# Four-tile scalings on VectorE, half of the inversion's loads from GpSimd, and other planner prices for SyncE, in a gated DeltaNet and S5 trunk

## The chip, the cores and the metric

The kernel runs on one core of a Trainium2 chip. The metric is the device time of one execution in microseconds. TensorE (PE) does the matmuls, VectorE (DVE) and ScalarE (ACT) the element-wise work, GpSimd (POOL) small element-wise work, memsets and some DMAs, and SyncE (SP) only issues DMAs. The engines run their own instruction lists in order and meet at semaphores.

## The reference, cut to what matters

The model has two layers. The first is the one that the change touches: a gated DeltaNet mixer with 8 heads of 128 channels over 1024 tokens, in chunks of 64, beside a memory attention, then an output projection, a layer norm and an MLP. Per head, with gc the cumulated log decay in a chunk:

```python
diff = gc[..., :, None] - gc[..., None, :]
decay = jnp.where(causal, jnp.exp(jnp.where(causal, diff, 0.0)), 0.0)
a_strict = jnp.where(strict, jnp.einsum('bhnid,bhnjd->bhnij', kb, k) * decay, 0.0)
sol = lax.linalg.triangular_solve(eye + a_strict, rhs, left_side=True, lower=True, unit_diagonal=True)
def step(state, inp):
    v_new = ui - jnp.einsum('bhcd,bhde->bhce', wi, state)
    attn = jnp.einsum('bhid,bhjd->bhij', qi, ki) * deci
    o = qi*exp(gci) @ state + attn @ v_new
    state = state * exp(g_last) + k_dec^T @ v_new
```

The second layer has an S5 state-space mixer in place of the DeltaNet, then the same attention, projection, norm and MLP. All matrices are float32.

## The kernel before, in words

A large float32 product is split into a high and a low float32r part on each side and done as three matmuls (lines 371 to 373); ACT makes the high part of a weight (L350) and DVE the low one (L351), from a raw tile that SP loads (L341). Small products are float32 matmuls. The tokens lie in 8 tiles of 128 rows; a "half" is four of them, so that a tile [128, 4, 128] is half a head.

The DeltaNet runs over heads. `gdn_recur(h)` is the serial recurrence: per token tile a chain ks (L1308) to R on DVE (L1310), pe (L1314) to e, copied by ACT (L1316), pS (L1320) to S on DVE (L1325). Beside it runs `gdn_fill(h + 1)`, which supplies the filling matmuls: the projections of head h + 1 and the keys of head h + 3, each as 24 matmuls of 128x512 per half.

For each half, `gdn_keys_out` makes the decay tile D: `decay` (L987 to L997) loads the cumulated sums, adds the causal mask on DVE (L994) and exponentiates on ACT, tile by tile with the token's own sum as the bias (L996). ACT sums squares for the norms (L1017), scales the keys to kd (L1026, stored to kdd, L1027) and scales D by gam, four tiles (L1029), stored to ded (L1030). DVE multiplies D with the key product kk (L1036) to NT (L1037), and ACT copies its diagonal blocks to pkd (L1041); GpSimd stores NT and pkd. `gdn_values_out` scales the transposed values by sk, four tiles on ACT (L1224).

For each pair of heads `gdn_inverse` inverts the 32x32 diagonal blocks on DVE (L1067 to L1114), and GpSimd stores them to t32 (called t in the profile). Per head, `gdn_invert_tiles` (L1127 to L1188) loads them into seven tiles, bz (L1146), two thirds of mz (m1, L1148, and m3, L1153), bv (L1149), the two halves of tv (tA, L1151, and vB, L1154), na (L1156) and the two result tiles TT, called iv (L1158), 34 loads per head by SP, all but na of 32x4x32 elements; then five groups of four small matmuls (`mm4`, L1163) with copies between them. `gdn_fill` decides after how much of the projection work these five groups are emitted: for heads 2, 4 and 6 they are held back by `wait` (22.0, in the loop over heads in `run`).

`run` ends by `settle`, a list scheduler over the whole program after the first weight. It prices each instruction (`price`), walks the five engines' lists, and fixes the order on each engine. A DMA on SP costs 0.33 us of its queue and one on GpSimd 0.65 us in that table; a tile that is written anew can start when its buffer is free. PE may take an instruction up to 40 us ahead of the plan (`reach`). So any change of a price can move instructions of all engines.

Of the kernel before, what the change touches and what calls it, by code (L numbers as in the profile page):

```python
# [16 lines left out]
P = 128  # L17
# [13 lines left out]
class Trunk:  # L31
# [26 lines left out]
    def settle(self, first, last, reach=0.0, ahead=15.0, passes=1, margin=0.0, late=0.0, hold=1e3):  # L58
# [118 lines left out]
        for _ in range(passes):  # L177
            due, now = [0.0] * n, 0.0
            place = {x: k for k, x in enumerate(turns)}
            for x in turns:  # L180
                due[x] = now
                now += cost[x][0]
            for x in reversed(range(n)):
                if ins[x].engine != E.PE:
                    due[x] = min([due[y] for y in after[x] + next_[x]] + [now + 50.0]) - lag - cost[x][1]


            slots, turn = {}, {}
            for x in range(n):
                for nm in fresh[x]:  # L190
                    turn.setdefault(self.home[nm][:2], []).append(nm)
            for t in turn:
                held = sum(1 for nm in users if self.home[nm][:2] == t and nm in before)
                slots[t] = [0.0] * (self.home[turn[t][0]][2] - held)
            todo = {nm: len(s) for nm, s in users.items()}
            over = {nm: 0.0 for nm in users}

            def room(x):
                t0, need = 0.0, {}
                for nm in fresh[x]:  # L200
                    need.setdefault(self.home[nm][:2], set()).add(nm)
                for t, s in need.items():
                    if set(turn[t][:len(s)]) != s or len(slots[t]) < len(s):
                        return None
                    t0 = max(t0, sorted(slots[t])[len(s) - 1])
                return t0


            free, locked, served, head, kind = {e: 0.0 for e in names}, 0.0, 0.0, 0, ""
            ready, wait = [0.0] * n, [len(d | f) for d, f in zip(deps, follow)]  # L210
            open_ = {e: [x for x in range(n) if ins[x].engine == e and not wait[x]] for e in names}
            order, lost, gone, table = [], 0.0, set(), 0
            while len(order) < n:
                first_ = None
                drift = free[E.PE] - due[turns[head]] if head < len(turns) else 0.0
                for e in names:
                    pick = None
                    for x in open_[e]:
                        if e == E.PE and x != turns[head] and due[x] > due[turns[head]] + reach - 1e-6:
                            continue  # L220
                        s = room(x) if fresh[x] else 0.0
                        if s is None:
                            continue
                        r = max(ready[x], s, free[e], due[x] - ahead if e != E.PE else 0.0)
                        if cost[x][2] > 1.5:
                            r = max(r, due[x] + drift - hold)
                        if e == E.PE and kind == "fr" and ins[x].ins[0].dtype == F32:
                            r += 0.15
                        other = 1.28 if sets[x] not in (None, table) else 0.0
                        k = (0, due[x] + other, r, x) if r <= free[e] + 0.1 else (1, r + other, due[x], x)  # L230
                        if pick is None or k < pick[0]:
                            pick = k, r, x
                    if pick and (first_ is None or pick[1:] < first_[1:]):
                        first_ = pick
                assert first_, f"no order: {len(order)} of {n}"
                r, x = first_[1:]
                e = ins[x].engine
                busy, length, moves = cost[x]
                if sets[x] not in (None, table):
                    table, busy, length = sets[x], busy + 1.28, length + 1.28  # L240
                if moves:
                    served = max(served, r + length - moves) + moves
                    length = served - r + late
                if port[x]:
                    r = max(r, locked)
                    locked = r + busy
                if e == E.PE:
                    lost += r - free[e]
                    kind = (kind + "fr"[ins[x].ins[0].dtype == F32R])[-2:]
                    gone.add(x)  # L250
                    while head < len(turns) and turns[head] in gone:
                        head += 1
                open_[e].remove(x)
                free[e] = r + busy
                order.append(x)
                for nm in fresh[x]:
                    t = self.home[nm][:2]
                    slots[t].remove(min(slots[t]))
                    turn[t].remove(nm)
                for y in after[x] + then[x]:  # L260
                    same = e == E.PE and ins[y].engine == e
                    ready[y] = max(ready[y], r + (0.0 if x not in deps[y] else busy if same else length + lag + (margin if ins[y].engine == E.PE else 0.0)))
                    wait[y] -= 1
                    if not wait[y]:
                        open_[ins[y].engine].append(y)
                for nm in uses(ins[x]):
                    if nm in users:
                        over[nm] = max(over[nm], r + length)
                        todo[nm] -= 1
                        if not todo[nm] and nm not in behind and self.home[nm][:2] in slots:  # L270
                            slots[self.home[nm][:2]].append(over[nm] + lag)
            if best is None or free[E.PE] < best[0]:
                best = free[E.PE], order
            turns = [x for x in order if ins[x].engine == E.PE]
# [5 lines left out]
    def price(self, i, big):  # L280

        E = mybir.EngineType
        if i.opcode == "DMACopy":
            def run(ap):
                k = 1
                for s, c in reversed(ap):
                    if s != k:
                        break
                    k *= c
                return 4 * k  # L290

            q = [x.bass_ap.ap for x in (i.ins[0], i.outs[0])]
            size, k = 4e-3 * math.prod(c for s, c in q[1]), min(run(a) for a in q)
            moves = size / (300 if k >= 2048 else 230 if k >= 512 else 150 if k >= 256 else 90 if k >= 128 else 40)
            return (0.33 if i.engine != E.Pool else 0.65), 1.6 + size / 300 + (0.0 if k >= 512 else 0.7), moves
        if i.engine == E.PE:
            if i.ins[0].dtype == F32R:
                return 0.014 + 0.416e-3 * big, 0.39 if big > 256 else 0.29, 0
# [690 lines left out]
    def decay(self, h, hf, tag):  # L989

        nc = self.nc
        pb = self.sums(h, hf, tag)
        d = self.tile(tag, [P, 4, P], F32, "D")
        nc.vector.tensor_tensor(d, pb, self.maskneg.unsqueeze(1).to_broadcast([P, 4, P]), op=ALU.add)  # L994
        for t in range(4):
            nc.scalar.activation(d[:, t, :], d[:, t, :], AF.Exp, bias=self.ngc[:, 4 * hf + t, h:h + 1])  # L996
        return d  # L997

    def gdn_keys(self, h, xT, w=None):
# [3 lines left out]
    def gdn_keys_out(self, h, hf):  # L1003
# [21 lines left out]
        for t in range(4):  # L1025
            nc.scalar.activation(kd[:, t, :], pt[:, t, :], AF.Copy, scale=self.kds[:, 4 * hf + t, h:h + 1])  # L1026
        nc.sync.dma_start(self.kdd[h, hf], kd)  # L1027
        for t in range(4):
            nc.scalar.activation(d[:, t, :], d[:, t, :], AF.Copy, scale=self.gam[:, 4 * hf + t, h:h + 1])  # L1029
        nc.scalar.dma_start(self.ded[h, hf], d)  # L1030
        pq = self.psum("pa", "kk", (P, 4, P))
        n = self.tile("h1", [P, 4, P], F32, "NT")
# [94 lines left out]
    def gdn_invert_tiles(self, h):  # L1127
# [20 lines left out]
            load(m1[q32[k]], block(0, k // 2, 2 * (k % 2)))  # L1148
            load(bv[q32[k], :, q32[k]], block(1, k // 2, 2 * (k % 2) + 1))  # L1149
        for k in range(4):  # L1150
            load(tA[q32[k], :, q32[k % 2]], block(0, k // 2, k % 2))  # L1151
        for k in range(4):
            load(m3[q32[k]], block(1, k // 2, 2 * (k % 2) + 1))  # L1153
            load(vB[q32[k], :, q32[k % 2]], block(1, k // 2, 2 + k % 2))  # L1154
        for f in range(2):
            load(na[q64[f], :, q64[f]], self.ntf[h, f][0:64, :, 64:P])  # L1156
            for b in range(4):
                load(TT[f][q32[b], :, q32[b]], block(1, f, b))  # L1158

        def mm4(a, b, n):  # L1160
            ps = self.psum("pi", "iv", (P, 4, P))[:, :, 0:n]
# [54 lines left out]
    def gdn_values_out(self, h, hf):  # L1216
# [3 lines left out]
        pt = self.psum("pa", "vt", (P, 4, P))  # L1220
        for t in range(4):
            nc.tensor.transpose(pt[:, t, :], vT[hf][:, t * P:(t + 1) * P], self.ident)
        for t in range(4):
            nc.scalar.activation(vs[:, 4 * hf + t, :], pt[:, t, :], AF.Copy, scale=self.sk[:, 4 * hf + t, h:h + 1])  # L1224

    def gdn_gate(self, h, xT):

# [809 lines left out]
    def run(self):  # L2037
# [26 lines left out]
        self.mix = self.quad(F32, "mix")  # L2064
        self.take(fill, 1e9)
        for h in range(7):
            fill = self.gdn_fill(h + 1, xT, 22.0 if h % 2 else 0.0)
            self.weave(self.gdn_recur(h), fill, 2.75 if h < 5 else 1.95)
            self.take(fill, 1e9)
        x = a["x"].rearrange("(n s) d -> s n d", s=8)  # L2070
# [191 lines left out]
```

## Time and profile before

| | |
|---|---|
| median of 3 runs | 2602.24 us (2595.83 to 2606.0) |
| profiled execution | 2604.86 us, span 2603.1 us |
| busy: PE, DVE, ACT, POOL | 2522.5, 1941.7, 1294.7, 362.3 us |
| mean granted TensorE clock | 0.991 |
| PE not busy, 0 to 240 us | 19.2 us |
| PE not busy, 240 to 700 us (rest of the DeltaNet, start of the output projection) | 17.3 us |
| PE not busy, 700 to 2604 us (MLPs, S5 layer, norms) | 44.95 us |

The three last rows are the length of the stage less PE's busy time in it. In the lines of the profile a row names the source line, the engine, the operation, the tiles out<-in and their shape; times are from the start of the span.

### The profile page before, as it was taken

The numbers are of one execution on the slowest core, as the hardware profiler recorded it, in microseconds if no ns is written. First come the engines' busy times: TensorE is split into PE (matmuls) and PEld (weight loads), VectorE is DVE, ScalarE is ACT, GpSimd is POOL, SyncE is SP. The second block draws the span as 40 slices with busy tenths as digits, with TensorE's granted clock in tenths as the row PEclk, the third lists the DMA queues.
The fourth block names the chain that finished last, engine by engine and source line by source line (L and its number), as shares of the span: only waits on it lengthen the run. The fifth ranks groups of instructions, "written<-read, shape, count | busy, mean of one in ns | idle before, by whom it ended". The sixth has DMA issues, their size and how long they took to land.

```text
span 2603.1 us, 36577 instructions
## 1 busy us (share of the span) xinstructions
PE 2522.5 (97%) x12301; PEld 2093.2 (80%) x12301; DVE 1941.7 (75%) x3625; ACT 1294.7 (50%) x2901; POOL 362.3 (14%) x528
## 2 busy tenths in 40 slices
PE   7999999998999999999999999989999999999998
PEld 5888888887887788878888888878877888888886
DVE  6675757575759799979988956663768766578788
ACT  6666666564426457454444245663235455454441
POOL 1111212011003004221210222121012000000002
PEclk9999999999999999999999999999999999999999
DMA  5443444344423457577454478655313444574432
GB/s 186 118 119 98 106 115 111 99 136 120 150 89 109 169 184 253 190 268 250 133 168 135 159 234 235 195 160 170 115 65 138 163 160 163 198 262 149 146 106 93
DMA packets 278172, 404.57 MB, mean 155 GB/s; under 512 B 119856, under 2 KB 137472, under 8 KB 277984
## 3 DMA queue, kind: packets, MB, share of 16 engines
q1 hardware_dynamic: 256096, 349.30, 41.7%
q0 software_dynamic: 19584, 48.75, 6.3%
q10 hardware_dynamic: 2304, 4.20, 0.4%
q8 instruction: 97, 1.59, 0.3%
q14 instruction: 91, 0.75, 0.1%
HBM read 274.73 MB, written 127.37 MB: 154 GB/s over the span
## 4 chain that ended last, share of the span: by engine, by line
PE 75%; DVE 11%; ACT 4%; DMA 2%; issue 2%; POOL 2%; SPq 1%; POOLq 0%; DVEq 0%; ACTq 0%
PE q L372 6%; PE q L371 6%; PE q L373 6%; PE tm L371 3%; PE tm L373 3%; PE tm L372 3%; PE pB L371 3%; PE pB L372 3%; PE pB L373 3%; PE wi L371 2%; PE wi L373 2%; PE wi L372 2%; PE pC L371 2%; PE pC L372 2%; PE pC L373 2%
## 5 line engine op out<-in xcount | busy, mean ns | idle before, releaser
L371 PE MATMUL q<-wkh,hkh 128*128 128x512 f32 x784 | 306.4, 391 | 1.9 <-DVE z L1743 1.7
L372 PE MATMUL q<-wkl,hkh 128*128 128x512 f32 x784 | 305.8, 390 | 1.1 <-DVE wkl L782 1.1
L373 PE MATMUL q<-wkh,hkl 128*128 128x512 f32 x784 | 305.6, 390 | 0.0
L781 ACT CAST wkh<-wr 128x512 fp32r<-128x512 f32 x168 | 104.9, 624 | 242.2 <-PE q L372 192.9
L371 PEld LDWEIGHTS q<-wkh,hkh 128*128 128x128 f32 x784 | 147.2, 188 | 33.5 <-DVE z L1743 2.1
L372 PEld LDWEIGHTS q<-wkl,hkh 128*128 128x128 f32 x784 | 147.3, 188 | 32.2 <-DVE wkl L782 2.1
L373 PEld LDWEIGHTS q<-wkh,hkl 128*128 128x128 f32 x784 | 147.2, 188 | 30.3
L782 DVE TENSOR_TENSOR wkl<-wr,wkh 128x512 fp32r<-128x512 f32 x168 | 115.7, 689 | 63.4 <-issue 51.6
L371 PE MATMUL wi<-xTh,wih 128*128 128x512 f32 x384 | 159.6, 416 | 1.2 <-ACT qT L974 1.2
L373 PE MATMUL wi<-xTh,wil 128*128 128x512 f32 x384 | 155.7, 406 | 0.0
L372 PE MATMUL wi<-xTl,wih 128*128 128x512 f32 x384 | 154.8, 403 | 0.0
L486 POOL TENSOR_SCALAR mv<-mv 128x1 f32<-128x1 f32 x32 | 24.8, 776 | 873.6 <-DVE mv L485 632.6
L782 DVE TENSOR_TENSOR hkl<-hr,hkh 128x512 fp32r<-128x512 f32 x196 | 134.3, 685 | 2.8 <-ACT hkh L781 2.8
L1535 DVE TENSOR_TENSOR y<-tm,y 128x512 f32<-128x512 f32 x128 | 88.0, 689 | 60.3 <-PE tm L373 58.5
L781 ACT CAST hkh<-hr 128x512 fp32r<-128x512 f32 x196 | 121.0, 617 | 0.0
L371 PEld LDWEIGHTS wi<-xTh,wih 128*128 128x128 f32 x384 | 74.0, 193 | 13.3 <-ACT qT L974 1.6
L373 PEld LDWEIGHTS wi<-xTh,wil 128*128 128x128 f32 x384 | 73.5, 191 | 13.5
L372 PEld LDWEIGHTS wi<-xTl,wih 128*128 128x128 f32 x384 | 73.9, 192 | 12.1 <-issue 0.2
L775 DVE TENSOR_TENSOR y<-q,y 128x512 f32<-128x512 f32 x112 | 72.1, 683 | 0.0
L371 PE MATMUL tm<-ow,ok 128*128 128x512 f32 x160 | 63.7, 398 | 0.5 <-DVE y L1533 0.5
L373 PE MATMUL tm<-ow,ok 128*128 128x512 f32 x160 | 62.6, 391 | 0.0
L372 PE MATMUL tm<-ow,ok 128*128 128x512 f32 x160 | 62.3, 390 | 0.0
(550 smaller groups left out, 7467.9 us busy)
## 6 DMA issues: line engine op xcount, KB each, us to landing
hr<-hd SPq DMA_DIRECT2D x212, 256.0 KB, 2.7
wr<-in_w_dram SPq DMA_DIRECT2D x56, 512.0 KB, 5.1
hd<-u SPq DMA_DIRECT2D x92, 256.0 KB, 2.0
w1r<-in_w_dram SPq DMA_DIRECT2D x40, 512.0 KB, 3.7
w1r<-in_w_dram SPq DMA_DIRECT2D x64, 256.0 KB, 4.3
hd<-hid SPq DMA_DIRECT2D x60, 256.0 KB, 3.2
hd<-p SPq DMA_DIRECT2D x60, 256.0 KB, 2.5
wir<-in_w_in_dram SPq DMA_DIRECT2D x24, 512.0 KB, 3.3
```

Source lines behind the costliest of these rows:

```text
L371: mm(ps, a[0], b[0], start=start, stop=False, skip_group_check=onto)
L372: mm(ps, a[0], b[1], start=False, stop=False, skip_group_check=onto)
L373: mm(ps, a[1], b[0], start=False, stop=stop, skip_group_check=onto)
L486: nc.gpsimd.tensor_scalar(mv[:, 2:3], mv[:, 1:2], 1e-5, None, op0=ALU.add)
L775: V.tensor_tensor(o, bank[t], o, op=ALU.add)
L781: nc.scalar.copy(hi, s)
L782: nc.vector.tensor_tensor(lo, s, f32(hi), op=ALU.subtract)
L1535: nc.vector.tensor_tensor(y[c], ps, y[c], op=ALU.add)
```

## The change

The edits are these. The decay tile: DVE adds the token's sum and the mask in one instruction per tile (four of 128x128 in place of one of 128x512), and ACT exponentiates all four tiles in one instruction. The scaling of D by gam and that of the values by sk become one DVE product of 128x512 each, with the factor broadcast along the tile's last axis. The loads of tA, vB and TT, 16 of the 34 loads per head, are issued by GpSimd. In the planner SP's DMAs cost 0.45 us and GpSimd's 0.60 us, and a DMA on SP may start 1 us after its buffer is free. The wait ahead of the inversions of heads 2, 4 and 6 is 34.0 in place of 22.0.

```diff
@@ settle
                         s = room(x) if fresh[x] else 0.0
                         if s is None:
                             continue
+                        if e == E.SP:
+                            s += 1
@@ price
-            return (0.33 if i.engine != E.Pool else 0.65), 1.6 + size / 300 + (0.0 if k >= 512 else 0.7), moves
+            return (0.45 if i.engine != E.Pool else 0.6), 1.6 + size / 300 + (0.0 if k >= 512 else 0.7), moves
@@ decay
-        nc.vector.tensor_tensor(d, pb, self.maskneg.unsqueeze(1).to_broadcast([P, 4, P]), op=ALU.add)
         for t in range(4):
-            nc.scalar.activation(d[:, t, :], d[:, t, :], AF.Exp, bias=self.ngc[:, 4 * hf + t, h:h + 1])
+            nc.vector.scalar_tensor_tensor(d[:, t, :], pb[:, t, :], self.ngc[:, 4 * hf + t, h:h + 1], self.maskneg, op0=ALU.add, op1=ALU.add)
+        nc.scalar.activation(d, d, AF.Exp)
@@ gdn_keys_out
-        for t in range(4):
-            nc.scalar.activation(d[:, t, :], d[:, t, :], AF.Copy, scale=self.gam[:, 4 * hf + t, h:h + 1])
+        V.tensor_tensor(d, d, self.gam[:, t4, h].unsqueeze(2).to_broadcast([P, 4, P]), op=ALU.mult)
@@ gdn_invert_tiles
-            load(tA[q32[k], :, q32[k % 2]], block(0, k // 2, k % 2))
+            nc.gpsimd.dma_start(tA[q32[k], :, q32[k % 2]], block(0, k // 2, k % 2))
-            load(vB[q32[k], :, q32[k % 2]], block(1, k // 2, 2 + k % 2))
+            nc.gpsimd.dma_start(vB[q32[k], :, q32[k % 2]], block(1, k // 2, 2 + k % 2))
-                load(TT[f][q32[b], :, q32[b]], block(1, f, b))
+                nc.gpsimd.dma_start(TT[f][q32[b], :, q32[b]], block(1, f, b))
@@ gdn_values_out
-        for t in range(4):
-            nc.scalar.activation(vs[:, 4 * hf + t, :], pt[:, t, :], AF.Copy, scale=self.sk[:, 4 * hf + t, h:h + 1])
+        t4 = slice(4 * hf, 4 * hf + 4)
+        nc.vector.tensor_tensor(vs[:, t4, :], pt, self.sk[:, t4, h].unsqueeze(2).to_broadcast([P, 4, P]), op=ALU.mult)
@@ run
-            fill = self.gdn_fill(h + 1, xT, 22.0 if h % 2 else 0.0)
+            fill = self.gdn_fill(h + 1, xT, 34.0 if h % 2 else 0.0)
```

The order of PE's instructions moves in the first 620 us or so of its work and hardly behind that. Three places follow; in each row stand the line, the operation, the tiles and the shape.

The first is PE at the start, where the keys of the second head are turned (kt) and multiplied (kk). The products mk are the memory attention's keys, mv its values. Before, with the last row of mk_735 and the first of mk_768:

```order
L373 MATMUL mk_735<-memh_691,wkl_732 128x256
L1014 MATMUL kt_513<-ident,kT_268 128x128 x4
L1036 MATMUL kk_538<-kT_268 128x128 x4
L1014 MATMUL kt_560<-ident,kT_268 128x128 x4
L371 MATMUL mk_768<-memh_677,wkh_764 128x256
```

After, the end of the fourth mk and the first of mv (the two groups mk_756 and mk_789, 24 matmuls each, stand wholly ahead of kt):

```order
L375 MATMUL mk_789<-memh_679,wkl_786 128x256
L373 MATMUL mv_816<-wvh_820,memh_665 128x512
L374 MATMUL mv_816<-wvl_821,memh_665 128x512
L375 MATMUL mv_816<-wvh_820,meml_666 128x512
L373 MATMUL mv_816<-wvh_820,memh_665 128x512
L1016 MATMUL kt_507<-ident,kT_268 128x128 x4
L1037 MATMUL kk_529<-kT_268 128x128 x4
```

So 48 matmuls of 128x256 and four of 128x512 that stood behind kt now stand ahead of it.

The second is ACT in the recurrence of head 1, where the keys of head 4 are finished, up to the e of the fourth token tile. Before:

```order
L1030 DMA ded<-D_3085 128x512
L996 ACTIVATE D_3179<-D_3179,scr_80 128x128 x4
L1029 ACTIVATE D_3179<-D_3179,scr_80 128x128 x4
L1026 ACTIVATE kd_3199<-kt_3185,scr_80 128x128
L978 ACTIVATE th_3080<-qT_3022 128x512
L1041 COPY pkd_3217<-NT_3211 32x128
L1316 COPY e_3240<-pe_3238 128x128
```

After:

```order
L998 ACTIVATE D_3140<-D_3140 128x512
L1019 ACTIVATE jk,scr_80<-kt_3146 128x128
L980 ACTIVATE th_3044<-qT_2986 128x512
L973 COPY cv_2988<-wi_3095 128x512
L976 ACTIVATE qT_2987<-wi_3095,scr_80 128x512
L1031 DMA ded<-D_3049 128x512
L1031 DMA ded<-D_3140 128x512
L1028 ACTIVATE kd_3160<-kt_3146,scr_80 128x128 x3
L1042 COPY pkd_3175<-NT_3169 32x128
L1317 COPY e_3198<-pe_3196 128x128
```

The eight instructions on D before this e are one, and cv, qT and two more of the kd, which stood behind e, stand ahead of it. On PE this e is read by pS; between pe and that pS stood 2 filling matmuls of 128x512 before, and now 14 of them, four transposes and three matmuls of 128x128 stand there.

The third is SP at the end of recurrence 5, from the loads for head 6's inversion to kdl, the keys for recurrence 6. Before, the last rows of a stretch that begins with mz and bv for head 6 (30 further issues, from that mz on, stand ahead of the first row here):

```order
L1149 DMA bv_1960<-t_97 32x4x32 x2
L1146 DMA bz_1959<-ntf 32x4x32 x4
L1148 DMA mz_1964<-t_97 32x4x32 x4
L1149 DMA bv_1960<-t_97 32x4x32 x2
L1153 DMA mz_1964<-t_97 32x4x32
L1354 DMA cat_105<-oT_6176 1024x1x64
L341 DMA or_6841<-in_w_o_dram 128x1024
L2109 DMA y_6801<-in_x_dram 128x512
L2109 DMA y_6802<-in_x_dram 128x512
L1297 DMA kdl_6284<-kdd 128x512
```

After, all rows from head 6's first mz to kdl:

```order
L1149 DMA mz_1946<-t_97 32x4x32 x4
L1150 DMA bv_1942<-t_97 32x4x32 x4
L1154 DMA mz_1946<-t_97 32x4x32 x4
L1355 DMA cat_105<-oT_6047 1024x1x64
L343 DMA or_6745<-in_w_o_dram 128x1024
L2110 DMA y_6705<-in_x_dram 128x512
L2110 DMA y_6706<-in_x_dram 128x512
L1150 DMA bv_1942<-t_97 32x4x32 x4
L1147 DMA bz_1941<-ntf 32x4x32
L1298 DMA kdl_6194<-kdd 128x512
```

The loads of tv, iv and na are gone from this stretch, and three of head 7's four bz and its mz stand behind kdl. GpSimd's list now has the 16 loads per head between its stores, its memsets and its small powers (L1023, L1336 before).

## The prediction

> **What bounds the kernel now.** I read the page first, for the engine that fills the span, then PE's busy time by stage, then what PE waits for, and then the lists of the engines that it waits for.
>
> ```profile
> span 2603.1 us, 36577 instructions
> PE 2522.5 (97%) x12301; PEld 2093.2 (80%) x12301; DVE 1941.7 (75%) x3625; ACT 1294.7 (50%) x2901; POOL 362.3 (14%) x528
> ```
>
> PE is busy for 97% of the span, and the change neither adds nor removes a matmul. All that it can win is time in which PE waits, or runs at a lower clock after a wait. The table of stages says where that time lies (columns: stretch, its length, PE busy, granted clock, DMA share, GB/s):
>
> ```profile
> 240.00:700.00 460.00, 442.66 (x2466) 0.98 0.45 121
> 700.00:2604.00 1904.00, 1859.05 (x8664) 0.99 0.50 167
> ```
>
> Behind 700 us PE waits for 45 us, but the edited functions run in the DeltaNet alone, and PE's order behind it is nearly what it was. What can be won is among the waits ahead of 700 us. PE's waits name the large ones (total, times, longest):
>
> ```profile
> PE kt L1014 <- DVE kT L979: 7.1, 1, 7.1
> PE pS L1320 <- ACT e L1316: 4.4, 2, 2.2
> PE pS L1320 <- DMA kdl<-kdd: 3.9, 1, 3.9
> PE iv L1163 <- DMA mz<-t: 2.6, 1, 2.6
> ```
>
> That is 18.0 us in five places: A, kt at 60 us; B and C, pS at 314 and 451 us, the same step of recurrences 1 and 3; D, iv at 604 us; E, pS at 624 us. Behind each the granted clock is low:
>
> ```profile
> 60.00:63.00 3.00, 3.00 (x17) 0.56 0.82 303
> 315.00:318.00 3.00, 2.90 (x12) 0.54 0.83 251
> 452.00:456.00 4.00, 3.60 (x15) 0.50 0.76 221
> 456.00:460.00 4.00, 4.00 (x18) 0.68 0.47 117
> 604.00:608.00 4.00, 3.48 (x16) 0.67 0.29 55
> 624.00:630.00 6.00, 5.59 (x21) 0.56 0.26 49
> ```
>
> PE's busy time times what is missing of the clock is lost: 1.3 for A, 1.3 for B, 1.8 + 1.3 for C, 1.1 for D, 2.5 for E, together 9.3 us. So the five places cost 27.3 us, with their clock: A 8.4, B 3.5, C 5.3, D 3.7, E 6.4. This is what the change aims at, and about the most that it can win.
>
> **B and C: ScalarE's queue.** The first fence is PE's timeline at B, the second ACT's:
>
> ```profile
> 311.15 0.40 PE L373 MATMUL wi<-xTh,wil 128*128 128x512 f32 x1
> 313.77 0.49 PE L1320 MATMUL pS<-e,kdl 128*128 128x128 f32 x2 [2.22 <-ACT e L1316]
> ```
>
> ```profile
> 309.82 1.28 ACT L996 ACTIVATE D<-D,scr 128x128 f32<-128x128 f32 x4
> 311.23 1.28 ACT L1029 ACTIVATE D<-D,scr 128x128 f32<-128x128 f32 x4
> 312.41 0.35 ACT L1026 ACTIVATE kd<-kt,scr 128x128 f32<-128x128 f32 x1
> 313.47 0.25 ACT L1316 COPY e<-pe 128x128 f32<-128x128 f32 x1
> ```
>
> ACT copies e only after eight scalings on D that came due just then. The prices, from the groups by line and the burst's own stretch (PE, PEld, DVE, ACT, POOL):
>
> ```profile
> L996 ACT ACTIVATE D<-D,scr 128x128 f32<-128x128 f32 x64 | 21.6, 402 | 6.1 <-DVE D L994 6.0
> L1029 ACT ACTIVATE D<-D,scr 128x128 f32<-128x128 f32 x64 | 20.4, 397 | 0.2
> L1224 ACT ACTIVATE mix<-vt,scr 128x128 f32<-128x128 f32 x64 | 19.7, 376 | 0.2
> L978 ACT ACTIVATE th<-qT 128x512 f32<-128x512 f32 x16 | 10.1, 630 | 8.9 <-DVE qT L976 8.9
> L994 DVE TENSOR_TENSOR D<-gb,scr 128x512 f32<-128x512 f32 x16 | 11.0, 688 | 4.0 <-DMA gb<-gcd 4.0
> L1214 DVE TENSOR_TENSOR mix<-qk,Dq 128x512 f32<-128x512 f32 x16 | 11.0, 689 | 13.2 <-DMA Dq<-ded 13.1
> L1325 DVE SCALAR_TENSOR_TENSOR S<-S,scr,pS 128x128 f32<-128x128 f32 x48 | 16.5, 344 | 8.5 <-PE pS L1320 8.1
> 299.00:320.00 21.00, 18.16 (x93) 15.34 (x93) 18.91 (x39) 16.90 (x60) 9.04 (x11) 0.92 0.40 110
> ```
>
> Per half, ACT loses four Exp (21.6 / 16 = 1.35 us) and gains one of 128x512. That one does not stand in the trace; it is bounded by the short one, 0.40, below and by the four, 1.35, above, and I take 0.63 from the Tanh of the same shape. It loses gam's four (20.4 / 16 = 1.28) and the values' four (19.7 / 16 = 1.23): in all 3.2 us per half. DVE gains four of 128x128 where one of 128x512 stood: 4 x 0.344 - 0.69 = 0.69 us, by S, its nearest row in form; between nothing, if they overlap down to the one, and 4 x 0.69 - 0.69 = 2.1, if each cost a whole one. The two products cost as L994 and L1214, 0.69 each; a broadcast factor could at worst double that. So DVE gains 2.1 us per half, 33 us in 16 halves (22 to 78 by the bounds), and ACT loses 52. Neither is on PE's path but in the bursts, since PE has filling matmuls ready elsewhere; where that cover fails, DVE's part of a burst counts in full.
>
> In the burst around B two halves meet: ACT falls from 16.9 by 2 x (0.72 + 1.28) = 4.0 us of 21, and DVE rises from 18.9 by 2 x 1.38 = 2.8, to 21.7 of 21. So VectorE is full there, and late by 0.7 us or a little more, for S, R and the low weight parts behind it. Against that, the new order puts 14 matmuls of 128x512 between pe and pS where 2 stood. They cover well over the 2.2 us by which e was late; and it moves the inversions of heads 2, 4 and 6, with their copies, out of the burst. I take 1.5 us as what is left of each of B and C, clock included: **gain 2.0 + 3.8 = 5.8 us**.
>
> **D and E: SyncE's queue.** Its timeline from head 6's first load to kdl, and kdl's landing:
>
> ```profile
> 592.25 1.80 SPq L1148 DMA_DIRECT2D mz<-t  x4
> ...
> 603.53 1.20 SPq L1156 DMA_DIRECT2D na<-ntf  x2
> 604.84 3.86 SPq L1158 DMA_DIRECT2D iv<-t  x8
> ...
> 618.13 0.90 SPq L1297 DMA_DIRECT2D kdl<-kdd  x2
> DMA to landing us min/median/max: 2.8/4.6/6.3
> ```
>
> SP issues without a pause: mz x4 in 1.80 and iv x8 in 3.86 make 0.45 to 0.48 us per issue. In D the last of the m3 loads stands behind tA and vB and is issued about 603, 10.8 us after the first load. In the changed order the twelve loads of m1, bv and m3 stand together, 12 x 0.48 = 5.8 us. The matmul that waited for 2.6 us gets its operand 5 us sooner, if PE comes at the same time, so D goes but for a remnant that I put at 0.5: **gain 3.2 us**. In E, kdl had 46 issues ahead of it from the first mz on (25.9 us by the two ends above); it now has 20, some 9.6 us. But one of them is head 7's bz, whose buffer head 6's third iv has to have read; then bz and kdl are issued (2 x 0.48) and land in 2.8 to 6.3 us, before the pS that stands some 7 us of matmuls behind that iv. With the median, 4.6, it just fits; with 6.3 it is late. I leave 2.0 us: **gain 4.4 us**.
>
> What GpSimd takes on in exchange is 128 issues. Their price is bounded by its own rows, the 64 KB store below, 0.76, from above, and SP's 0.43 for the same load from below:
>
> ```profile
> L1042 POOL DMA_DIRECT2D ntd<-pkd x16: 752/760/810, 59.7 to 527.8; - x16
> L1158 SPq DMA_DIRECT2D iv<-t x64: 303/430/662, 169.3 to 632.9; - x64
> ```
>
> I take 0.76, the row of the same queue: 12 us per head, in about 70 us per head of which GpSimd is busy for under 20, so it costs PE nothing as long as loads and powers find each other's gaps (the last rival prices the other case). The Trainium skill ("SBUF — State Buffer", section "SBUF: two separate sides") speaks against this move: a DMA issued by GpSimd needs its cores to write descriptors, and a VectorE instruction in a two-port mode shuts them out. The row of L1042 does not bear that out here: 16 issues lie within 752 to 810 ns, with DVE busy for three quarters of the span. By the page's figures (some 0.62 us alone and 3.1 beside such an instruction, an estimate for this case) a head's loads would take up to 50 us; the sum stays with the row.
>
> **A: the start.** PE waits for the second head's kT, and stands with 48 products mk and four mv ready behind kt. By these rows mk starts 0.12 us apart and 128x512 0.23:
>
> ```profile
> 45.78 0.28 PE L373 MATMUL mk<-memh,wkl 128*128 128x256 f32 x1
> 45.90 0.28 PE L371 MATMUL mk<-memh,wkh 128*128 128x256 f32 x1
> ```
>
> So 48 x 0.12 + 4 x 0.23 = 6.7 of the 7.1 us is filled. But DVE has 1.4 us more per half ahead of that kT, and the weights for mk and mv come through one chain of raw tile, ACT and DVE. I leave 2 us of wait and half of the clock's 1.3: **gain 5.7 us**.
>
> **Elsewhere.** For heads 2, 4 and 6 the recurrence is now packed closer: after one iv, two steps follow with only two to four fillers between. Before, no row shows such a place; I charge 2 us in all, between 0 and 6 (six links, each a copy late by one DVE or ACT product of 0.63 to 0.69, with a little clock). In the last attention of the S5 layer ACT switches tables twice more (Exp and Gelu alternate):
>
> ```profile
> L1434 ACT ACT_TABLE_LOAD x6 | 7.7, 1283 | 1.1 <-DVE mx L1431 1.1
> ```
>
> That is 2.6 us of ACT, mostly under matmuls that are ready; I charge 1.5. SP's higher price and its 1 us shift loads elsewhere without changing PE's order; nothing, give or take 3.
>
> **The sum.** 5.8 + 3.2 + 4.4 + 5.7 = 19.1, less 3.5, is 15.6 us. The profiled execution took 2604.9 us and would take 2589.3; it lies 2.6 above the median of 2602.2, so I predict 2602.2 - 15.6 = **2586.6 us**, -0.6%.
>
> **The rivals.**
>
> *VectorE takes ScalarE's place.* DVE is at 18.9 of 21 us in the burst before it gets 2.8 more; if its waits for Exp come on top, S and R are as late as e was, B and C stay (their 5.8 is lost) and the closely packed steps cost 5 in place of 2. For it: those 90%. Against it: the 14 fillers. 19.1 - 5.8 - 6.5 = 6.8 gained: 2595.
>
> *The loads aren't what is late.* The kdl row lands in up to 6.3 us, and the start's weights may come no sooner. Then D and E give 3, A gives 2, B and C 3, and the new costs stand: 8 - 5.5, some 2.5 gained: 2600, no change that can be told (a measurement of this kernel tells about 0.5%, 13 us, from none).
>
> *Slower: GpSimd's queue.* The power that a finished half needs (L1336) stands behind eight loads of tv for the next head, and these wait for that head's predecessor to be read by PE. If PE reads it late, the eight take 8 x 0.76 = 6.1 us ahead of the power, ACT's on and the single buffer of po; from 2.5 us of lateness on, PE waits. In heads 2, 4 and 6, with 3 us of clock each: 27 us lost against 19 won and 3.5 of other costs: 2614. The page named above would make this one likelier; the even 0.76 of L1042 makes it less so.
>
> **How the numbers follow.** Forecast 0.60, VectorE 0.20, loads 0.12, GpSimd 0.08. The best case wins all 27.3 us and costs nothing: 2575; I put the low end there. The high end takes in the second rival with 3 us for the shifted loads: 2603. Beyond lie the slower rival and a little. Faster by over 0.5% is under 2589: most of the forecast and little of the first rival, 0.56; slower by over 0.5% is above 2615: half of the last rival and a remnant, 0.06; the rest, 0.38, within.
>
> **What would show it.** Right: kt's wait under 3 us, no pS waiting for e by over 1 us near 315 and 450, D and E gone from PE's waits, fewer stretches at half clock ahead of 700 us, and behind 700 us PE's wait still about 45. Wrong: PE waiting for R or S on DVE, or for po behind on and L1336; kdl landing late; new waits in the MLPs, which I hold unchanged.

## The result and the profile after

The changed kernel takes 2582.3 us in the median of four runs (2580.1 to 2583.9), the kernel before beside it 2600.2 (2595.8 to 2606.0): a ratio of 0.9929, with a 95% interval of 0.9907 to 0.9951. That is 17.9 us, 0.7%, where 15.6 were forecast. The two profiled executions lie further apart, 2604.9 and 2580.1 us: that of before is on the slow side of its median, that of after the fastest of its four.

Page of the changed kernel, span and busy times:

```profile
span 2578.4 us, 36563 instructions
PE 2514.8 (98%) x12301; PEld 2084.7 (81%) x12301; DVE 1959.9 (76%) x3705; ACT 1255.8 (49%) x2727; POOL 429.6 (17%) x656
```

PE has the same 12301 matmuls and is busy for 7.7 us less, at a mean clock of 0.996 in place of 0.991; the other 17.0 of the 24.7 us of span are idle time. ACT lost 39 us and DVE gained 18, less than the 52 and 33 forecast; POOL gained 67. PE's largest waits in the first 700 us (total, times, longest), the first of them the program's start:

```profile
PE ba L889 <- ACT xTh L870: 8.7, 1, 8.7
PE po L1312 <- ACT on L1340: 3.4, 4, 1.5
PE ks L1309 <- DVE S L1324: 2.2, 3, 1.6
PE ot L1351 <- ACT iv L1180: 1.8, 2, 0.9
PE mv L374 <- DVE wvl L353: 1.1, 1, 1.1
```

The waits for kT, mz and kdl are gone, and that of pS for e but for 0.4 us. Grown are the waits of po for on (1.0 us before) and of ks for S (0.8 before). Where the time came from is seen by following one matmul, pS, in both kernels (duration in ns, then the start of the first and of the last). Before:

```profile
L1320 PE MATMUL pS<-e,kdl x112: 270/273/582, 215.6 to 720.9; 128*128 128x128 f32 x112
```

After:

```profile
L1321 PE MATMUL pS<-e,kdl x112: 270/273/377, 209.0 to 700.1; 128*128 128x128 f32 x112
```

So 6.6 us are won ahead of the first recurrence, and 14.2 more up to the end of the last one: 20.8 in the DeltaNet, and 3.9 behind it, where none was forecast.

To place this more finely in all kernels, PE's work is taken as a ruler: each matmul counts with the median distance to the next start for its shape (about 2460 us in all, the same in every kernel), and at equal work the starts in two traces are compared. This table has, for the trace of each kernel against that of before, the us won (-) or lost (+) between marks of that work: up to 265 us (A), 265 to 330 (B), 330 to 500 (C), 500 to 700 (D and E), and from there to the end; then the sum, and the ratio of the timed runs with its interval. "only" is the kernel before with one part of the change, "no" the changed kernel without it.

| kernel | A | B | C | D, E | rest | sum | ratio of times |
|---|---|---|---|---|---|---|---|
| changed | -6.3 | -3.2 | -3.6 | -7.5 | -4.0 | -24.6 | 0.9929 (0.9907-0.9951) |
| only_plan | -4.2 | -1.9 | -2.9 | -7.0 | -1.8 | -17.8 | 0.9952 (0.9940-0.9964) |
| only_price | +1.2 | +2.3 | +1.8 | -5.4 | +1.0 | +0.9 | 0.9999 (0.9990-1.0008) |
| only_margin | -0.6 | +0.7 | +0.4 | -4.4 | +0.5 | -3.4 | 1.0004 (0.9995-1.0013) |
| only_alu | -4.7 | -0.6 | -1.3 | -1.9 | +6.0 | -2.5 | 1.0000 (0.9991-1.0009) |
| only_loads | -0.9 | -1.9 | -1.3 | -5.9 | +1.7 | -8.3 | 0.9973 (0.9964-0.9982) |
| only_wait | -0.6 | +7.7 | +6.6 | -2.8 | -2.7 | +8.2 | 1.0066 (1.0051-1.0081) |
| no_plan | -7.8 | -2.1 | +1.8 | -10.6 | +1.2 | -17.5 | 0.9941 (0.9929-0.9953) |
| no_alu | -3.2 | -3.9 | -3.5 | -9.7 | +3.1 | -17.2 | 0.9940 (0.9927-0.9954) |
| no_loads | -5.0 | -0.5 | -1.0 | -3.7 | -3.9 | -14.1 | 0.9952 (0.9940-0.9964) |
| no_wait | -5.7 | -1.6 | -1.8 | -9.7 | +8.5 | -10.3 | 0.9969 (0.9959-0.9979) |
| xsp | -6.4 | -4.2 | -3.8 | -8.3 | -4.3 | -27.0 | 0.9905 (0.9891-0.9918) |
| port4 | -8.8 | -0.3 | -0.3 | -8.1 | +2.9 | -14.6 | 0.9946 (0.9933-0.9960) |

Each row is one profiled execution, and executions of one kernel differ by some us (before: 2595.6 to 2607.5 in one set of 22), so differences of 1 or 2 us between rows are left unread. The ratio is taken against executions of before beside that kernel (median 2600.2 us beside the changed kernel, 2602.3 to 2603.5 beside the others), so a difference of two kernels' medians below can be off by 2 or 3 us. Of the four kernels without one part, only no_wait has an interval clear of the changed kernel's.

B and C hold more than the waits of pS for e. Before, PE also waits 1.56 us at 333 us for ACT's copy of a step of the inversion (in this line, with a short one elsewhere):

```profile
PE iv L1163 <- ACT iv L1179: 1.9, 2, 1.6
```

No other kernel has that wait there, so every row of column B holds about 1.6 us that have nothing to do with e.

### The profile page after: what moved, and what is told of

Read it like the earlier page. It is cut to its first block, busy times and chain, and to the rows that moved or that the text cites. A ratio compares the mean times of both kernels' runs of the same rounds, so it can differ in the third digit from the quotient of the medians.

```text
span 2578.4 us, 36563 instructions
## 1 busy us (share of the span) xinstructions
PE 2514.8 (98%) x12301; PEld 2084.7 (81%) x12301; DVE 1959.9 (76%) x3705; ACT 1255.8 (49%) x2727; POOL 429.6 (17%) x656
## 4 chain that ended last, share of the span: by engine, by line
PE 83%; DVE 7%; ACT 5%; issue 2%; POOL 2%; DMA 1%; SPq 0%; ACTq 0%; POOLq 0%; DVEq 0%
PE q L374 7%; PE q L373 7%; PE q L375 7%; PE tm L375 4%; PE tm L373 4%; PE tm L374 3%; PE pB L373 3%; PE pB L375 3%; PE pB L374 3%; PE wi L373 2%; PE wi L374 2%; PE wi L375 2%; PE pC L373 2%; PE pC L374 2%; PE pC L375 2%; PE pA L373 2%
## 5 line engine op out<-in xcount | busy, mean ns | idle before, releaser
L375 PEld LDWEIGHTS wi<-xTh,wil 128*128 128x128 f32 x384 | 72.5, 189 | 14.6
```

The costliest lines, as they stand in the source:

```text
L375: mm(ps, a[1], b[0], start=False, stop=stop, skip_group_check=onto)
```

## The experiments

### Each part alone

**only_plan**, the planner's three numbers:

```diff
+                        if e == E.SP:
+                            s += 1
-            return (0.33 if i.engine != E.Pool else 0.65), ...
+            return (0.45 if i.engine != E.Pool else 0.6), ...
```

> The kernel before with nothing but the planner's edits (SyncE's DMA 0.45 us, GpSimd's 0.60 us, 1 us of margin on SyncE's loads). Its order has 48 products mk and four mv ahead of kt at the start, as the changed kernel has; pe and pS of recurrence 1 stand with no filling matmul between them, and SyncE issues the same loads. Theory of parts (each edit wins its own place): the wait for kT at 60 us goes, 6 us, and the four others stay or get 1 us worse: 2594. Rival (the gains come from the planner's order as a whole, the operations matter little): most of the 20 us that the first 640 us have won come with it: 2582 to 2586.

2589.2 us, 13 less: between the two. Two thirds of A and nearly all of D, E are won, though no load has moved to GpSimd. SyncE's list in its trace shows how:

```profile
600.87 1.53 SPq L1150 DMA_DIRECT2D mz<-t  x3
602.45 0.43 SPq L1299 DMA_DIRECT2D kdl<-kdd  x1
602.92 0.43 SPq L1150 DMA_DIRECT2D mz<-t  x1
603.45 0.57 SPq L1356 DMA_DIRECT2D cat<-oT  x1
604.07 0.66 SPq L1299 DMA_DIRECT2D kdl<-kdd  x1
```

With a dearer DMA the planner puts kdl ahead of head 7's bv, tv and na, and in time. The queue need not be shortened for E; it can be put in another order. The waits for e stay, and are longer:

```profile
PE pS L1322 <- ACT e L1318: 6.5, 2, 3.2
```

That B and C are ahead all the same, by 1.9 and 2.9 us, has other causes: in B the wait at 333 us is gone, and in C the clock stays whole behind the wait (1.00 from 446 to 450 us, where 0.50 followed before).

**only_price** and **only_margin**, its two halves (the prices; the `s += 1`):

> The kernel before with nothing but the two DMA prices of the planner (SyncE 0.45, GpSimd 0.60 us). Its order keeps kt at the start ahead of the mk, but puts kdl 7 near 620 us ahead of head 7's bv, tv and na, as both prices and margin together do. Theory now (the price moves SyncE's loads, the margin moves kt): A stays, D and E go, 7 us: 2594. Rival (the margin does the work in both places): nothing goes, 2600.

> The kernel before with nothing but the 1 us of margin on SyncE's loads. Its order at the start is that of both planner's edits together, kt behind 48 mk and four mv, so that A goes, 4 us; SyncE's loads near 600 to 624 us stand nearly as before. Theory now: 4 to 6 us, 2596. Rival (the margin does the work in both places): 13 us, 2589.

2604.9 and 2602.9 us: nothing by either, where both together win 13. The theory of then is refuted (4 to 7 us each), and so are the rival's 13 us for the margin. Each half wins its place and loses as much elsewhere. With the prices alone D, E win 5.4 us, kt waits as before, and kdl is late in recurrences, three times:

```profile
PE kt L1014 <- DVE kT L979: 7.1, 1, 7.1
PE pS L1320 <- DMA kdl<-kdd: 5.0, 3, 2.6
```

With the margin alone kt is in place and 5 us are won; kk's wait for kd at 178 us, with what stands around it, takes them back by 190 us:

```profile
PE kk L1038 <- ACT kd L1028: 3.4, 2, 2.8
PE pS L1322 <- DMA kdl<-kdd: 2.3, 1, 2.3
```

Why the two together avoid both is not settled.

**only_alu**, the element-wise edits, shown here by their first:

```diff
-        nc.vector.tensor_tensor(d, pb, self.maskneg.unsqueeze(1).to_broadcast([P, 4, P]), op=ALU.add)
-            nc.scalar.activation(d[:, t, :], d[:, t, :], AF.Exp, bias=self.ngc[:, 4 * hf + t, h:h + 1])
+            nc.vector.scalar_tensor_tensor(d[:, t, :], pb[:, t, :], self.ngc[:, 4 * hf + t, h:h + 1], self.maskneg, op0=ALU.add, op1=ALU.add)
+        nc.scalar.activation(d, d, AF.Exp)
```

> The kernel before with nothing but the element-wise edits (mask and sum on VectorE, one Exp for four tiles, the scalings by gam and sk as VectorE products). Planner's prices, wait and loads are the old ones. Theory of parts: e is copied in time in recurrences 1 and 3, so that the two waits of pS for e go, 7 us with the clock; at the start its order puts 46 mk ahead of kt, 5 us; iv behind mz and pS behind kdl near 604 and 624 us stay: 2588. Rival (the order behind the longer wait is what wins there): pe and pS have eight fillers between them in place of 14 and the inversions stay in the burst, so that the two waits stay or go to VectorE: 2595.

2602.4 us: no change, and a miss of the theory of parts by 14 us. e is in time, but B and C stay, now as a wait for qT in the same burst:

```profile
PE wi L371 <- ACT qT L974: 6.6, 2, 3.3
```

What stands behind that is shown with no_wait, which has the same wait.

**only_loads**, the 16 loads by GpSimd:

```diff
-            load(tA[q32[k], :, q32[k % 2]], block(0, k // 2, k % 2))
+            nc.gpsimd.dma_start(tA[q32[k], :, q32[k % 2]], block(0, k // 2, k % 2))
```

> The kernel before with nothing but the 16 loads per head issued by GpSimd. Theory of parts: iv no longer waits for mz nor pS for kdl near 604 and 624 us, 7 us; kt at 60 us and e in recurrences 1 and 3 stay as they are: 2593. Rival (the loads weren't what was late, it is the landing or the order): 0 to 2 us, 2599. Rival (GpSimd's queue holds up the powers): slower, 2605.

2594.8 us, 7.5 less: the time of the theory of parts, but not all of its mechanism. kt's 7.1 and e's 4.4 us stand as they did, and iv's wait for mz went from 2.6 to 0.3; but kdl is still late, at 612 us:

```profile
PE pS L1320 <- DMA kdl<-kdd: 2.9, 1, 2.9
```

33 issues still stand ahead of it from head 6's first mz on, head 7's bz, mz and bv among them. So shortening the queue did not cure E's wait; the order on it has to change too. No wait of PE points at GpSimd's queue.

**only_wait**, 34.0 for 22.0:

```diff
-            fill = self.gdn_fill(h + 1, xT, 22.0 if h % 2 else 0.0)
+            fill = self.gdn_fill(h + 1, xT, 34.0 if h % 2 else 0.0)
```

> The kernel before with nothing but 34.0 in place of 22.0 ahead of the inversions of heads 2, 4 and 6. Its order has eight wi, four transposes and three products between pe and pS in recurrences 1 and 3, without a change of any instruction. Theory of parts: the wait alone wins little, since ScalarE's queue is as long as it was, and the recurrences behind it are packed closer: 2598 to 2602. Rival (the order is what wins): the two waits for e go, 7 us, with no edit of an instruction: 2593.

2619.6 us, 17 more: outside both. The waits for e did go, by order alone, but the loads come too late for the packed steps:

```profile
PE pS L1320 <- DMA kdl<-kdd: 9.4, 2, 5.1
PE po L1311 <- ACT on L1339: 4.9, 5, 1.6
PE iv L1163 <- DMA mz<-t: 4.1, 4, 2.5
```

### All but one part

From here two theories stood against each other: that each edit wins its own place, and that the longer wait wins B and C by its order, if SyncE's queue has been freed.

**no_wait** (22.0 in the changed kernel):

> The changed kernel with 22.0 in place of 34.0 ahead of the inversions of heads 2, 4 and 6. Theory of parts (the one on record: the element-wise edits win B and C): nothing is lost there and the closely packed steps of heads 2, 4 and 6 go, 2 us: 2580. Rival formed on the first four runs (the longer wait wins B and C by its order, if GpSimd has the loads): PE waits again in recurrences 1 and 3, for e or for what stands behind it, 3 us each with the clock: 2588 or more.

2593.7 us. The rival holds in its place: B and C win 3.4 us together, not 6.8. PE waits for qT, ACT for DVE, and DVE for hardly anybody (stretch, length, busy PE, PEld, DVE, ACT, POOL):

```profile
295.00:310.00 15.00, 11.46 (x60) 9.47 (x59) 14.52 (x37) 8.97 (x28) 7.86 (x11) 0.98 0.29 74
```

```profile
309.56 0.79 PE L373 MATMUL wi<-xTh,wih 128*128 128x512 f32 x1 [3.32 <-ACT qT L976]
```

```profile
308.30 0.63 ACT L980 ACTIVATE th<-qT 128x512 f32<-128x512 f32 x1 [1.68 <-DVE qT L978]
```

VectorE is busy for 14.5 of 15 us there, and qT is late behind its other work. This is the first rival of the prediction: with the scalings moved and the burst left as it was, VectorE takes ScalarE's place. But a full VectorE alone makes no wait. This is the changed kernel in the same 15 us, within 1 us of the same place in PE's work:

```profile
295.00:310.00 15.00, 15.00 (x86) 12.83 (x85) 14.72 (x35) 11.76 (x40) 4.49 (x6) 1.00 0.30 115
```

VectorE is as full, and PE has 86 matmuls to do in place of 60. So the wait of 34.0 does not empty the burst; it leaves PE work beside it. Head 2's inversion has its first matmul behind the burst in any case, at 321.2 us before and at 321.5 us in the changed kernel.

**no_loads** (all loads by SyncE):

> The changed kernel with all 34 loads per head by SyncE. Theory of parts: only D and E come back, iv behind mz near 604 us and pS behind kdl near 624 us, 7 us: 2589. Rival (the longer wait needs SyncE's queue freed): pS waits for kdl and iv for mz and bv in recurrences 2, 4 and 6, as with the longer wait alone, where 10 us were lost behind head 2's inversion and 8 behind head 4's: 2600 or more.

2589.2 us, some 7 above the changed kernel, the size that the theory of parts has, and not the 18 of the rival. But it is not all in D and E, which lose 3.8: B and C lose 5.3, 2.8 of it in two waits of pS for kdl, at 352 and 489 us. In D iv waits 1.1 us for mz; kdl near 624 us, which the theory of parts had late, is in time:

```profile
PE pS L1321 <- DMA kdl<-kdd: 2.8, 2, 1.6
```

**no_alu** (ScalarE's scalings as before):

> The changed kernel with the old element-wise instructions (eight scalings on D and four on the values per half on ScalarE). Theory of parts: B and C come back, 6 to 7 us, as pS waiting for e: 2589. Rival (the order wins B and C): e is in time, since the new order keeps 15 matmuls between pe and pS; ScalarE's longer queue costs 2 us at most: 2584.

2585.6 us, 3 above. B and C keep all their gain, 3.9 and 3.5 us, and no wait of pS for e is left. PE's waits from 300 to 330 us are these two:

```profile
PE po L1313 <- ACT on L1341: 0.7, 1, 0.7
PE qk L1215 <- ACT kd L1028: 0.6, 1, 0.6
```

So the relief of ScalarE is not what won them; the order is. What no_alu loses is in A, where mk waits 3.5 us for kv as in only_plan, and behind the DeltaNet.

**no_plan** (the planner's old numbers):

> The changed kernel with the planner's old prices for SyncE and GpSimd and no margin. Its order has 46 mk ahead of kt at the start, put there by the element-wise edits. Theory of parts: A is lost with the prices, 5.7 us: 2588. Rival (the place of kt has two causes, either is enough): A stays, and the time is within 3 us of the changed kernel's: 2583. A kdl or mz that is late near 620 us would show that the margin had a share in D and E.

2587.4 us. The time is that of the theory of parts, but A is not what is lost: it stays, as the rival has it, since kt's place has two sufficient causes. D and E stay too, and no kdl or mz is late near 620 us. C is lost, and the rest. In C it is mz that comes late, at 457 us, and the clock behind it is 0.57 from 458 to 464 us:

```profile
PE iv L1162 <- DMA mz<-t: 1.6, 1, 1.6
```

### The power for on

Of the waits that grew, that of po for on has a cause which the changed kernel's trace shows. POOL, with on's power at L1337:

```profile
310.89 0.83 POOL L1126 DMA_DIRECT2D t<-X  x1 [0.49 <-ACT X L1122]
311.74 1.75 POOL L1337 TENSOR_TENSOR scr<-scr,mhalf 128x4 f32<-128x4 f32 x1
```

DVE at that time:

```profile
311.38 1.22 DVE L353 TENSOR_TENSOR wzl<-wzr,wzh 128x1024 fp32r<-128x1024 f32 x1
```

The power stands behind a store of an inverted block (X), and then takes 1.75 us where 1.04 is the median. PE waits for it:

```profile
314.71 0.49 PE L1312 MATMUL po<-S,gb 128*128 128x128 f32 x2 [1.52 <-ACT on L1340]
```

The same stands at 445.9 us. **xsp** moves those stores:

```diff
-            nc.gpsimd.dma_start(dst[1][:, 8 * y:8 * y + 8, 16:32], Tt[q])
-            nc.gpsimd.dma_start(dst[0][:, 16:32, 8 * y:8 * y + 8], Tn[q])
+            nc.sync.dma_start(dst[1][:, 8 * y:8 * y + 8, 16:32], Tt[q])
+            nc.sync.dma_start(dst[0][:, 16:32, 8 * y:8 * y + 8], Tn[q])
```

> The changed kernel with the last four stores of an inverted block pair (X, 64x16x8 and 64x8x16) issued by SyncE in place of GpSimd. In the changed kernel the power for on stands behind one of them near 311 and 445 us, and PE waits 1.5 us twice for on. Theory now (GpSimd's queue and the shared port make the power late): the power no longer stands behind a store, the two waits of po go with their clock, 2 to 3 us each: 2577. Rival (the port alone makes it late): the power still ends 0.7 us late and at most half is won: 2581. If the loads of t32 come later by it, SyncE's queue gives it back: 2584.

2579.2 us, the fastest kernel here: 0.9905 of before (0.9891 to 0.9918). That is 3 us better than the changed kernel by medians of separate sets, and the two intervals overlap. The power starts 0.9 us earlier and takes its own time:

```profile
310.85 1.03 POOL L1337 TENSOR_TENSOR scr<-scr,mhalf 128x4 f32<-128x4 f32 x1 [1.44 <-DVE scr L1336]
```

```profile
PE wz L373 <- ACT vT L976: 2.5, 2, 1.2
PE po L1312 <- ACT on L1340: 0.8, 3, 0.5
```

3.4 us of po's waits became 0.8, but 2.5 us of wz's for vT stand behind them: some 2 us are left as a gain in the DeltaNet.

**port4** tells the planner instead that such a power uses the port of VectorE and GpSimd:

```diff
-            port.append(shared and (i.engine == E.DVE or big >= 8) and ...
+            port.append(shared and (i.engine == E.DVE or big >= 4) and ...
```

> The changed kernel with one number of the planner changed: a power of 128x4 on GpSimd counts as a user of the port that VectorE and GpSimd share (threshold 4 in place of 8 elements). Theory now: the planner puts the powers where VectorE leaves the port, they take 1.0 us and not 1.75, the waits of po for on near 313 and 447 us get shorter by 1 us each: 2579. Rival (a plan that differs anywhere moves the MLP and the S5 layer by as much as it wins here): within 6 us of the changed kernel, 2576 to 2588, with the DeltaNet's part alone better.

2590.0 us, 8 more than the changed kernel by the medians and 4 by the ratios, and a miss of both: the powers near 309 and 446 us still take 1.46, and po still waits for 2.9 us in all. Right behind, wz waits 0.9 us twice for vT, and then the clock halves, as it does not in the changed kernel (port4, then the changed kernel):

```profile
452.00:458.00 6.00, 6.00 (x21) 5.13 (x21) 3.42 (x9) 2.29 (x11) 3.14 (x6) 0.52 0.20 30
452.00:458.00 6.00, 6.00 (x40) 5.33 (x39) 5.16 (x11) 3.23 (x12) 6.00 (x12) 1.00 0.54 102
```

Against the changed kernel B and C lose 6.2 us together and the stages behind the DeltaNet 6.9; A wins 2.5. A truer number in the planner gave no better plan.

### What moves behind the DeltaNet

The column "rest" runs from -4.3 to +8.5, though none of the edited instructions stands there. PE's order is nearly the same; those of DVE and SyncE differ by plan. In no_wait, the worst, DVE's list at 1021 to 1030 us:

```profile
1021.18 0.68 DVE L550 TENSOR_TENSOR s4l<-s,s4h 128x512 fp32r<-128x512 f32 x1
1025.14 0.29 DVE L1715 TENSOR_SCALAR s5b<-s5b,sg 128x128 f32<-128x128 f32 x1 [3.28 <-DMA s5b<-in_b_dram]
1027.41 0.29 DVE L1716 TENSOR_SCALAR co<-co,sg 128x128 f32<-128x128 f32 x1 [1.98 <-DMA co<-in_c_dram]
...
1029.98 0.69 DVE L658 TENSOR_TENSOR u<-pB,p 128x512 f32<-128x512 f32 x1
```

```profile
PE pB L373 <- DVE u L658: 4.5, 1, 4.5
```

The planner has put preparations of the S5 layer between two steps of the MLP; their loads are late, and u, for which PE waits, stands behind them on DVE. This was read in the trace and not taken away by an experiment.

## Why the prediction was right, and where it was not

The time lies in the range and near the forecast. Its terms stand below against the table. They are read from one pair of executions that lie 24.8 us apart, where the medians lie 17.9 apart, so in all they are up to 7 us too large.

- **A**, 5.7: 6.3 measured. The fillers ahead of kt are the cause as it had it: kt's wait is gone in every kernel whose order has them there, and stands at 7.1 us in the three that have not (only_price, only_loads, only_wait).
- **B and C**, 5.8: 6.8 measured, some 1.6 of it from the wait at 333 us, which the prediction did not price. Of the two reasons that the prediction gave, the fillers between pe and pS and the relief of ScalarE, the runs bear out the first: without the relief all of it stays (no_alu), with the relief alone 1.9 us come (only_alu), none of them where pS stood, since PE waits there 3.3 us twice for qT. The relief counted as the remedy for "ScalarE's queue"; that step is wrong. That VectorE would be full, and that fillers would cover it, was right (stretch, length, busy PE, PEld, DVE, ACT, POOL):

```profile
291.00:312.00 21.00, 21.00 (x118) 17.88 (x117) 20.69 (x47) 14.22 (x51) 7.43 (x9) 1.00 0.40 104
```

  That the new order takes head 2's inversion out of the burst is not what the traces show: it stands behind it, before as after (321 us). The order needs the loads in time as well: with the wait alone B and C lose 14 us.
- **D and E**, 3.2 + 4.4: 7.5 measured, and 5.9 by the loads alone. For D the mechanism holds: with the loads alone mz's wait falls from 2.6 to 0.3 us. For E it is not enough: kdl's falls only from 3.9 to 2.9. A plan with the loads on SyncE wins 7.0 in D and E (only_plan): "SyncE's queue" was the place, and its order a remedy of its own. (By the lists kdl had 47 issues ahead of it and has 21, not 46 and 20; that changes nothing.)
- **Closely packed steps**, -2.0: too small. At PE's work of 275 to 285 us B is 5.0 us ahead of what it was, and gives 1.6 back at po and what follows; C gives back 2.4 in the same way, and near 505 us 2.4 more go. The three make 6.4 us. The gains beside them were larger in proportion, so that the net fits. Two errors met, and that is luck.
- **GpSimd's queue**, the rival at 27 us: not as stated. The power does stand behind a DMA, but behind the store of X and not the loads of tv, and the two waits of PE are 1.5 us each (they are part of the 6.4 above). With all loads on SyncE they are the same (no_loads, 3.4 us in four waits), so the moved loads are not their cause.
- **Prices.** Four products on D were put at 4 x 0.344. Three of them take 0.86 in no_wait's trace, 0.26 apart from start to start:

```profile
304.00 0.86 DVE L997 SCALAR_TENSOR_TENSOR D<-gb,scr 128x128 f32<-128x128 f32 x3
```

  That explains 3 of the 15 us by which DVE's gain of 18 falls short of 33: all 64 take 18.7 us in the changed kernel where 22.0 were forecast, and the new rows less L994's make 29.7. The rest was not taken apart; busy time counts overlapping instructions once, and the rows on D overlap (0.26 apart, 0.34 long). The Exp of 128x512, put at 0.63, takes 0.632 in the median; GpSimd's loads, put at 0.76, take 0.549.
- **Table loads**, -1.5: the two more did come, and that stretch was about 2 us faster all the same, mostly by its clock (0.62 from 1703 to 1712 us before, 0.81 from 1696 to 1705 after).
- **Behind 700 us nothing**: wrong. PE's order says little there, since DVE's and SyncE's orders move too. The changed kernel drew -4.0; other plans drew up to +8.5.
- **The second rival's sum** takes 5.5 for the new costs, which the forecast puts at 3.5; with these it would have come to 2598 and not 2600.

The change was priced as a whole, in its own order, and that helped. The nearness of the sum is in part luck all the same: in the traces the DeltaNet wins 20.8 us where 15.6 were forecast, and the 4.0 behind it were not foreseen. A sum of the parts would have missed: alone, the four parts measure -13, 0, -7.5 and +17 us, which makes -3.5, and together -18. Without one of them 9 to 17 us of gain remain.

## What to carry to other kernels

In a kernel whose whole order comes from a planner, an edit's gain is that of the order it leads to: price it in the new order, and leave room for stages that the edit does not touch (here -4 to +9 us). Here a wait on a full engine did not go by moving its work to the next fullest; it went when PE had more matmuls ready beside the same burst. Two remedies for one wait did not add, and a remedy that packs work closer needed its loads early first.

## What the runs showed of the hardware

The granted clock does not follow the length of a wait alone. In only_plan the same wait of pS for e, 3.2 us long, stands at 310 and at 446 us; behind the first the clock was half for part of the next 4 us, behind the second it was not:

```profile
311.00:315.00 4.00, 4.00 (x21) 3.77 (x20) 2.74 (x7) 2.81 (x12) 1.46 (x2) 0.57 0.87 267
446.00:450.00 4.00, 4.00 (x29) 3.59 (x28) 2.88 (x7) 3.79 (x15) 1.11 (x2) 1.00 0.85 275
```

So a wait of that length may or may not cost 1.7 us more (4.00 x 0.43); that part of the spread of the timed runs comes from there is not shown. The clock records of the traces show one thing more: the stretches at half clock begin on a grid of 3.41 us. In before four of them begin at 315.2, 451.8, 605.4 and 622.4 us, which are 40, 45 and 5 such steps apart, and each lasts one or two steps. In only_plan a point of the grid (444.4 us) parts the second wait into 1.9 and 1.3 us, while 2.4 us of the first lie within one step. That fits, but gives no rule: the step from 441.0 us, with PE busy for 1.45 of 3.4 us, had no half clock behind it, and steps with 1.65 in port4 had.

The power on GpSimd is held by a VectorE instruction that has both inputs in SBUF. The power that began 0.86 us ahead of the end of DVE's L353 took 1.75, those that began 0.57 ahead of one of L978 took 1.46: what was left, and 0.89 us. In xsp one of 1.77 us at 564.6 had no DMA within 19 us ahead of it, so the store is not the cause of its length. Beside a VectorE instruction with an input in PSUM nothing was held: this one began 0.64 us ahead of the end of L1038, which reads kk.

```profile
241.11 1.00 POOL L1337 TENSOR_TENSOR scr<-scr,mhalf 128x4 f32<-128x4 f32 x1 [1.56 <-DVE scr L1336]
```

The Trainium skill ("SBUF — State Buffer", section "SBUF: two separate sides") says that the port pair of VectorE and GpSimd is locked for a whole instruction, also where VectorE's has two SBUF inputs and GpSimd's reads SBUF; these rows agree. What the same section says of DMAs that GpSimd issues, and what the prediction weighed, does not show for these loads:

```profile
L1159 POOL DMA_DIRECT2D iv<-t x64: 548/549/602, 162.3 to 604.9; - x64
```

All 64 take 548 to 602 ns, with DVE busy for 76% of the span. Whether a VectorE instruction in a two-port mode stood beside them the profile does not say.
